# Other sizes for the seven pieces of a streaming kernel's last row

## Chip, cores and metric

The kernel runs on one core of a Trainium2 chip. The metric is the device time of one execution in microseconds (us).

## The reference

```python
log_input: float32 [1024, 4096]
target:    float32 [1024, 4096]

def reference(log_input, target):
    loss = np.exp(log_input) - target * log_input
    return np.mean(loss, axis=-1).astype(np.float32)
```

## The kernel before

Each of the 128 partitions holds eight rows of the batch. log_input (x) and target (t) stream in over one DMA queue. ScalarE takes exp(x) with its row sum, VectorE takes the product t*x with its row sum. The rows come in loads of four rows, two rows and one row; the last row comes in seven pieces, so that the arithmetic left after the last byte is small. A unit in this text is 32 columns, a 128th of a row, 16 KB over 128 partitions; "x98" is an x piece of 98 units.

```python
TAIL = [("x", 98), ("t", 50), ("t", 48), ("x", 24), ("t", 18), ("x", 6), ("t", 12)]
# ... cut: views, buffers, semaphores
for what, w in TAIL:
    loads.append((what, at[what], w * d // 128))
    at[what] += w * d // 128
# ... cut: all loads are issued in this order from SyncE, each with its own semaphore;
#     the last t load, the last exponential and the last but one product all count last_ready up
# VectorE, for each t piece (lo, w, i):
    x_load = next(ix for a, wx, ix in x_work if a + wx >= lo + w)   # the x piece that covers it
    if j == 0 or x_load > t_work[j - 1][2]:
        nc.vector.wait_ge(landed[x_load], 16)
    if j < n_t - 1:
        nc.vector.tensor_tensor_reduce(...).wait_op(landed[i], 16, "sem-ge")     # L175
    else:   # the last product also adds up the six partial sums of the row
        # ... cut: waits for the earlier partial sums
        nc.vector.tensor_tensor_reduce(...).wait_op(last_ready, 18, "sem-ge")    # L193
```

Of the kernel before, what the change touches and what calls it, by code (L numbers as in the profile page):

```python
# [7 lines left out]
F32 = mybir.dt.float32  # L8


TAIL = [("x", 98), ("t", 50), ("t", 48), ("x", 24), ("t", 18), ("x", 6), ("t", 12)]


def before_first_barrier(nc, instructions):
# [16 lines left out]
def kernel(tc, log_input, target, out):  # L31
# [33 lines left out]
    at = {"x": last_row * d, "t": last_row * d}  # L65
    for what, w in TAIL:
        loads.append((what, at[what], w * d // 128))
# [175 lines left out]
```

## Time and profile before

| | before |
|---|---|
| time, three runs | 84.07 us (84.00 to 84.13) |
| span of the profiled run | 82.5 us |
| VectorE, ScalarE busy | 43%, 40% |
| DMA queue busy | 95.8% |

How to read it: in the profile DVE is VectorE, ACT is ScalarE, SPq is SyncE's queue of DMA issues; a READ_ACCUMULATOR line, one column wide, follows each product (0.08 us) and each exponential (0.19 us), for which the kernel asks for a row sum. Both engines idle for more than half of the span, and the queue hardly at all, so shares say nothing about the tail; only start times do. In the timeline a line has the start, the duration, the engine and source line, the operation, and in brackets the idle time before it with what ended it. Three lines that the prediction does not show serve below as marks: the first product of the whole kernel, the product of the row before the last, and the exponential of the last row's large x piece.

```profile
41.12 4.43 DVE L175 CUSTOM_DVE_ANT_0 t_big<-t_big,x_big 128x4096 f32<-128x4096 f32 x1 [41.12 <-DMA t_big<-in_target_dram]
...
70.33 4.43 DVE L175 CUSTOM_DVE_ANT_0 t_big<-t_big,x_big 128x4096 f32<-128x4096 f32 x1 [1.00 <-DMA t_big<-in_target_dram]
...
74.10 2.79 ACT L155 ACTIVATE e_dump<-x_big 128x3136 f32<-128x3136 f32 x1 [4.44 <-DMA x_big<-in_log_input_dram]
```

All three start when their load lands. They tell when the stream reached a given byte in this run.

### The profile page before, as it was taken

How to read it: one execution, taken by the hardware profiler on the slowest of the kernel's cores; microseconds unless marked ns; L12 is line 12 of the kernel's file. 1: busy time of each engine (PE TensorE's matmuls, PEld its weight loads, DVE VectorE, ACT ScalarE, POOL GpSimd, SP SyncE). 2: the span in 40 equal slices, each digit the busy share in tenths (PEclk: the TensorE clock that was granted, in tenths of full speed). 3: DMA queues.
4: the chain of work that ended last, by engine and by line, in shares of the span. 5: the costliest groups of instructions: out<-in, count | busy, mean ns of one | idle time of the engine just before them, and what ended most of it. 6: DMA issues, size and time to landing. Idle time of an engine off the chain costs nothing.

```text
span 82.5 us, 131 instructions
## 1 busy us (share of the span) xinstructions
DVE 35.6 (43%) x22; ACT 33.2 (40%) x35; POOL 0.3 (0%) x5
## 2 busy tenths in 40 slices
DVE  0000000000000000000099999999369995993992
ACT  0500000000499920000000998979792496009460
POOL 0000000000000000000000000000000000000000
DMA  9289999929999992999599799799799999999960
GB/s 508 127 381 508 508 508 508 476 95 445 508 508 508 508 413 95 508 508 508 254 508 429 333 508 492 318 460 508 302 453 397 461 421 418 426 402 412 397 231 2
DMA packets 2016, 33.56 MB, mean 407 GB/s; under 512 B 352, under 2 KB 608, under 8 KB 1120
## 3 DMA queue, kind: packets, MB, share of 16 engines
q1 hardware_dynamic: 2016, 33.56, 95.8%
HBM read 33.55 MB, written 0.00 MB: 407 GB/s over the span
## 4 chain that ended last, share of the span: by engine, by line
DMA 72%; DVE 18%; issue 5%; SPq 3%; DVEq 0%
DMA t_big<-in_target_dram 49%; DMA x_big<-in_log_input_dram 23%; DVE t_big L175 17%; SPq L129 3%; DVE t_big L193 1%; DVE parts L175 0%; DVEq L192 0%; SPq L127 0%; DVE all_loss L193 0%
## 5 line engine op out<-in xcount | busy, mean ns | idle before, releaser
L175 DVE CUSTOM_DVE_ANT_0 t_big<-t_big,x_big 128x4096 f32<-128x4096 f32 (+3 forms) x8 | 26.2, 3308 | 43.5 <-DMA t_big<-in_target_dram 43.4
L155 ACT ACTIVATE e_dump<-x_big 128x4096 f32<-128x4096 f32 (+3 forms) x8 | 21.8, 2729 | 23.9 <-DMA x_big<-in_log_input_dram 23.6
L141 ACT ACTIVATE join_dump<-parts 128x2 f32<-128x2 f32 x7 | 1.4, 203 | 20.4 <-DVE parts L175 20.3
L175 DVE CUSTOM_DVE_ANT_0 t_mid<-t_mid,x_mid 128x4096 f32<-128x4096 f32 x2 | 8.8, 4424 | 2.0 <-DMA t_mid<-in_target_dram 2.0
L155 ACT ACTIVATE e_dump<-x_mid 128x4096 f32<-128x4096 f32 x2 | 7.1, 3568 | 0.0
L155 ACT ACT_TABLE_LOAD x1 | 1.3, 1283 | 2.9 <-PEq L48 2.9
L155 ACT ACTIVATION_READ_ACCUMULATOR e_dump<-x_big 128x1 f32 x8 | 1.5, 186 | 0.0
L141 ACT ACTIVATION_READ_ACCUMULATOR join_dump<-parts 128x1 f32 x7 | 1.3, 186 | 0.0
L175 DVE DVE_READ_ACCUMULATOR2_ANT parts<- 128x1 f32 x7 | 0.6, 84 | 0.0
L193 DVE CUSTOM_DVE_ANT_0 t_big<-t_big,x_big 128x390 f32<-128x390 f32 x1 | 0.6, 566 | 0.0
L155 ACT ACTIVATION_READ_ACCUMULATOR e_dump<-x_mid 128x1 f32 x2 | 0.4, 186 | 0.0
L175 DVE DVE_READ_ACCUMULATOR2_ANT t_big<- 128x1 f32 x3 | 0.2, 82 | 0.0
L136 POOL MEMSET x_big<- 128x6 f32 x1 | 0.1, 104 | 2.5 <-POOLq L48 2.5
L227 POOL MEMSET const-uint8-127<- 128x1 uint8 x1 | 0.1, 102 | 0.0
L227 POOL MEMSET const-bfloat16-1.0<- 128x1 bf16 x1 | 0.1, 101 | 0.0
L227 POOL MEMSET const-float32-0.0<- 128x1 f32 x1 | 0.1, 98 | 0.2 <-issue 0.2
L227 POOL MEMSET const-float32-1.0<- 128x1 f32 x1 | 0.1, 98 | 0.0
L193 DVE DVE_READ_ACCUMULATOR2_ANT all_loss<- 128x1 f32 x1 | 0.1, 82 | 0.0
## 6 DMA issues: line engine op xcount, KB each, us to landing
x_mid<-in_log_input_dram SPq DMA_DIRECT2D x1, 4096.0 KB, 49.9
t_mid<-in_target_dram SPq DMA_DIRECT2D x1, 4096.0 KB, 59.2
x_big<-in_log_input_dram SPq DMA_DIRECT2D x1, 2048.0 KB, 19.8
t_big<-in_target_dram SPq DMA_DIRECT2D x1, 2048.0 KB, 24.3
x_big<-in_log_input_dram SPq DMA_DIRECT2D x1, 1568.0 KB, 15.4
t_big<-in_target_dram SPq DMA_DIRECT2D x1, 800.0 KB, 17.0
t_big<-in_target_dram SPq DMA_DIRECT2D x1, 768.0 KB, 18.4
x_big<-in_log_input_dram SPq DMA_DIRECT2D x1, 384.0 KB, 18.9
```

Of the source, the lines that this page charges most:

```text
L129: dma = nc.sync.dma_start(out=place(what, lo, w), in_=src[:, lo : lo + w])
L136: nc.gpsimd.memset(big["x"][:, 4 * d : 4 * d + n_parts], -1.0).then_inc(ones_done, 1)
L141: nc.scalar.activation(out=join_dump[:, 2 * row : 2 * row + 2], in_=parts[:, 2 * row : 2 * row + 2], func=ACT_F.Copy, scale=inv_d, accum_o ...
L155: nc.scalar.activation(out=e_dump[:, col : col + w], in_=place("x", lo, w), func=ACT_F.Exp, bias=0.0, scale=1.0, accum_out=parts[:, 2 * ro ...
L175: nc.vector.tensor_tensor_reduce(out=place("t", lo, w), in0=place("t", lo, w), in1=place("x", lo, w), scale=-1.0, scalar=0.0, op0=ALU.mult ...
L193: nc.vector.tensor_tensor_reduce(out=place("t", lo, w + n_parts), in0=place("t", lo, w + n_parts), in1=place("x", lo, w + n_parts), scale= ...
L227: nc = _bacc.Bacc("TRN2", target_bir_lowering=False, num_devices=1)
```

## The change

Only the sizes of the last row's pieces change; their order, their number and their total stay. To judge by the sizes, the intent is rounder pieces: all x pieces (3200, 768 and 128 columns of 4 bytes) become whole multiples of 512 bytes a partition.

```diff
-TAIL = [("x", 98), ("t", 50), ("t", 48), ("x", 24), ("t", 18), ("x", 6), ("t", 12)]
+TAIL = [("x", 100), ("t", 50), ("t", 50), ("x", 24), ("t", 16), ("x", 4), ("t", 12)]
```

## The prediction

> **What bounds the kernel now.** I read the page first. ScalarE and VectorE are each busy for well under half of the span, and the DMA queue carries 33.56 MB at almost its full share, so the kernel is a stream of loads with the arithmetic beside it:
>
> ```profile
> span 82.5 us, 131 instructions
> DVE 35.6 (43%) x22; ACT 33.2 (40%) x35; POOL 0.3 (0%) x5
> q1 hardware_dynamic: 2016, 33.56, 95.8%
> ```
>
> The change alters neither the bytes nor the number of loads, so the body of the stream cannot gain. What can move is the short stretch at the end, in which the last row arrives in seven pieces. The page's list of issues gives the time from issue to landing, and the chain in order of time gives the issue times 59.06, 59.53, 60.02, 60.52 and 61.04; the timeline has the first issue (x of 98 units) at 58.69 and the last at 61.52. (A unit is 32 columns, one 128th of a row, so 16 KB over 128 partitions.)
>
> ```profile
> x_big<-in_log_input_dram SPq DMA_DIRECT2D x1, 1568.0 KB, 15.4
> t_big<-in_target_dram SPq DMA_DIRECT2D x1, 800.0 KB, 17.0
> t_big<-in_target_dram SPq DMA_DIRECT2D x1, 768.0 KB, 18.4
> x_big<-in_log_input_dram SPq DMA_DIRECT2D x1, 384.0 KB, 18.9
> t_big<-in_target_dram SPq DMA_DIRECT2D x1, 288.0 KB, 19.2
> t_big<-in_target_dram SPq DMA_DIRECT2D x1, 192.0 KB, 18.9
> x_big<-in_log_input_dram SPq DMA_DIRECT2D x1, 96.0 KB, 18.9
> ```
>
> Adding the two gives landings, each good to about 0.05 us: x98 74.09, t50 76.06, t48 77.93, x24 78.92, t18 79.72, x6 79.94, t12 80.42. Against these stands the timeline of the end (start, duration, instruction):
>
> ```profile
> 76.05 1.83 DVE L175 CUSTOM_DVE_ANT_0 t_big<-t_big,x_big 128x1600 f32<-128x1600 f32 x1 [1.28 <-DMA t_big<-in_target_dram]
> 77.80 0.08 DVE L175 DVE_READ_ACCUMULATOR2_ANT t_big<- 128x1 f32 x1
> 77.94 1.76 DVE L175 CUSTOM_DVE_ANT_0 t_big<-t_big,x_big 128x1536 f32<-128x1536 f32 x1
> 78.93 0.81 ACT L155 ACTIVATE e_dump<-x_big 128x768 f32<-128x768 f32 x1 [1.53 <-DMA x_big<-in_log_input_dram]
> 79.62 0.08 DVE L175 DVE_READ_ACCUMULATOR2_ANT t_big<- 128x1 f32 x1
> 79.68 0.19 ACT L155 ACTIVATION_READ_ACCUMULATOR e_dump<-x_big 128x1 f32 x1
> 79.70 0.76 DVE L175 CUSTOM_DVE_ANT_0 t_big<-t_big,x_big 128x576 f32<-128x576 f32 x1
> 79.97 0.33 ACT L155 ACTIVATE e_dump<-x_big 128x192 f32<-128x192 f32 x1
> 80.24 0.19 ACT L155 ACTIVATION_READ_ACCUMULATOR e_dump<-x_big 128x1 f32 x1
> 80.38 0.08 DVE L175 DVE_READ_ACCUMULATOR2_ANT t_big<- 128x1 f32 x1
> 80.50 0.57 DVE L193 CUSTOM_DVE_ANT_0 t_big<-t_big,x_big 128x390 f32<-128x390 f32 x1
> ```
>
> What to see: the product of t48 starts at 77.94, just as its data land, 0.06 us after the previous accumulator read ended (77.88). From there VectorE runs without a hole that matters: 77.94 to 79.70, 79.70 to 80.46, and the last instruction at 80.50. That last one waits for three things at once, and all three come within 0.04 us: ScalarE's last read (80.24 + 0.19 = 80.43), the landing of t12 (80.42) and VectorE's own previous piece (80.46). The old sizes balance the tail so finely that anything moved later on one of the three arms shows in full, while moving one of them earlier gains nothing.
>
> [...]
>
> **The change part by part.** It adds no instruction and removes none. Every piece still needs the same x loads, there are still six partial sums, and t12 with its 390-column last instruction is as before.
>
> *Landings.* From x98's landing (74.10, where its exponential starts) to t48's (77.94) 800 + 768 KB came in 3.84 us, which is 418 GB/s, or 0.039 us for a unit. All loads run through one queue in order of issue, so a landing moves by the change in the sum of units up to it. The sums were 98, 148, 196, 220, 238, 244, 256 and become 100, 150, 200, 224, 240, 244, 256. So x100 and the first t50 land 0.08 us later, the second t50 0.16 later, x24 0.16 later, t16 0.08 later, and x4 and t12 where x6 and t12 did.
>
> *VectorE.* The first t50 starts at 76.05 + 0.08 = 76.13 and is over, accumulator read and all, at 77.96 (1.83 later). The second t50 lands at 77.93 + 0.16 = 78.09, so VectorE now stands still for some 0.1 us and starts at 78.10. It has 1600 columns for 1536, 1.826 us for 1.759 (the two durations on the page), and ends at 79.93. t16 has landed at 79.80 and starts at once. [...] It ends at 80.62. The last instruction starts 0.04 us later, as before, at 80.66 for 80.50.
> The sum is simpler than the steps: from the second large t piece on VectorE works through 1536 + 576 = 2112 columns before and 1600 + 512 = 2112 after, in the same number of instructions. So the shift of the end is the shift of that piece's landing, 4 units x 0.039 = 0.16 us; the 64 columns that the piece gained are given back by t16.
>
> *ScalarE.* x24 starts at 78.93 + 0.16 = 79.09 and its read at 79.84. The next ACTIVATE can start 0.09 us after a read has started (45.70 and 45.79 in the timeline), at 79.93; x4 lands only at 79.94, so it starts at 79.97 as x6 did. [...] so its read ends at about 80.38 instead of 80.43. This arm gets 0.05 us shorter, which buys nothing.
>
> *Path that sets the end.* VectorE 80.62, t12 80.42, ScalarE 80.38. VectorE alone sets it, +0.16 us. The output store and the rest follow unchanged. 84.07 + 0.16 = 84.23 us, +0.19%.
>
> **Rivals.**
> 1. The stream sets the end, the time stays at 84.07. For it: the DMA queue is 95.8% busy, and t12 lands where it did. Against it: in the tail VectorE has no slack, its own piece ended 0.04 us after t12 landed already before. It would need the second t50 to start early, and it cannot, for it starts on landing.
> 2. ScalarE becomes the last arm: x24 is late, its read pushes x4. By the steps above there is 0.01 us between read and landing, so a small delay of x24 does pass on. But x4 would have to start 0.25 us late to pass VectorE (80.38 + 0.25 = 80.63). An extra delay of that size would bring some 84.3; I see nothing that causes it.
> 3. The transfers get faster or slower with the sizes. The two middle pieces now end at multiples of 512 B in the row (3200 columns are 12800 B, 3136 were 12544 B), and the small ones are 2048 and 512 B. The tail already runs below 418 GB/s in its small pieces (96 and 288 KB between 78.92 and 79.94, which is 386 GB/s), so size matters a little. If round sizes helped by a few per cent on the 200 units up to the second t50, which take 8 us, it would land 0.1 to 0.2 us earlier and the result would be 84.0 to 84.1[...]. Against it: the first t50 (6400 B, not a multiple of 512) and t48 (6144 B, one) came at the same rate, 800 KB in 1.95 us and 768 KB in 1.89, 420 and 416 GB/s.
>
> **Range and chances.** The three runs of before lie within 0.13 us, as large as the effect, and the landings are known to 0.05 us. With rivals 1 and 3 on the low side and 2 and 3 on the high side I take 84.03 to 84.42. Two per cent are 1.68 us, ten times the largest shift found in any arm, so within 2% has 0.98, and the rest is split evenly.
>
> **What would show it.** In the profile after: t products of 1600, 1600, 512 and 390 columns at some 1826, 1826, 692 and 566 ns; a wait of about 0.1 us on the target's load before the second 1600; no wait before the 512; the last instruction about 0.2 us after ScalarE's last read and after t12's landing, released by VectorE's own read. Wrong would be a last instruction that starts at 80.5 with the second 1600 no later than 77.96 (then the landings did not move by units), or one that waits for ScalarE or for t12's load.

The forecast's sum came to 84.07 + 0.16 = 84.23 us, with VectorE at 80.62 ahead of t12 (80.42) and ScalarE (80.38); two of its terms are 0.692 us for the product of 512 columns and 0.281 us for the exponential of 128. Both can be estimated from the profile of before alone (`--lines --by-form`). Products of 1600, 1536 and 576 columns took 1826, 1759 and 759 ns, so a column costs (1826 - 1759)/64 = 1.047 ns and 512 columns 759 - 64 x 1.047 = 692 ns. Exponentials of 768 and 192 columns took 815 and 334 ns, so a column costs 481/576 = 0.835 ns and 128 columns 334 - 64 x 0.835 = 281 ns.

## The result

| | before | after |
|---|---|---|
| median of six runs | 84.02 us (83.98 to 84.13) | 84.14 us (83.98 to 84.22) |
| ratio after/before | | 1.0011, 95% interval 0.9998 to 1.0024 |
| span of the profiled run | 82.5 us | 82.8 us |

A ratio is the mean time of one kernel's fast runs over that of the other's of the same rounds, so it is not quite the ratio of the medians quoted. The clock alone does not settle that anything changed: the interval reaches to 1. The profile does, if it is read with care. The same lines of the timeline of the changed kernel:

```profile
41.31 4.43 DVE L175 CUSTOM_DVE_ANT_0 t_big<-t_big,x_big 128x4096 f32<-128x4096 f32 x1 [41.31 <-DMA t_big<-in_target_dram]
...
70.53 4.43 DVE L175 CUSTOM_DVE_ANT_0 t_big<-t_big,x_big 128x4096 f32<-128x4096 f32 x1 [1.01 <-DMA t_big<-in_target_dram]
...
74.37 2.84 ACT L155 ACTIVATE e_dump<-x_big 128x3200 f32<-128x3200 f32 x1 [4.52 <-DMA x_big<-in_log_input_dram]
...
76.33 1.82 DVE L175 CUSTOM_DVE_ANT_0 t_big<-t_big,x_big 128x1600 f32<-128x1600 f32 x1 [1.37 <-DMA t_big<-in_target_dram]
...
78.08 0.08 DVE L175 DVE_READ_ACCUMULATOR2_ANT t_big<- 128x1 f32 x1
78.29 1.82 DVE L175 CUSTOM_DVE_ANT_0 t_big<-t_big,x_big 128x1600 f32<-128x1600 f32 x1
...
80.04 0.08 DVE L175 DVE_READ_ACCUMULATOR2_ANT t_big<- 128x1 f32 x1
80.04 0.69 DVE L175 CUSTOM_DVE_ANT_0 t_big<-t_big,x_big 128x512 f32<-128x512 f32 x1
80.18 0.28 ACT L155 ACTIVATE e_dump<-x_big 128x128 f32<-128x128 f32 x1
80.40 0.19 ACT L155 ACTIVATION_READ_ACCUMULATOR e_dump<-x_big 128x1 f32 x1
80.65 0.08 DVE L175 DVE_READ_ACCUMULATOR2_ANT t_big<- 128x1 f32 x1
80.77 0.57 DVE L193 CUSTOM_DVE_ANT_0 t_big<-t_big,x_big 128x390 f32<-128x390 f32 x1
```

The last product starts at 80.77 for 80.50, 0.27 us later. But the first product of the kernel, far ahead of anything that changed, already starts 0.19 us later (41.31 for 41.12). That part is the stream of this one run. What is left for the change is 0.27 - 0.19 = 0.08 us.

A better mark lies closer: the start of the large exponential, at which x98 or x100 has landed. The time from there to the last product is 80.50 - 74.10 = 6.40 us before and 80.77 - 74.37 = 6.40 after; x100 is two units larger and so should itself land 2 x 0.039 = 0.08 us later (0.039 us a unit is 3.84 us for 98 units, from 74.10 to 77.94 before), which puts it at 6.48 on the scale of before. Again +0.08 us, but all of it is this correction, so it has to be checked: from the product of the row before to the large exponential it is 74.10 - 70.33 = 3.77 us before and 74.37 - 70.53 = 3.84 after, 0.07 more.

The landings moved as the prediction said. In the list of issues (us from issue to landing) the two t50 pieces now share one line with their median, and t12 has the other:

```profile
t_big<-in_target_dram SPq DMA_DIRECT2D x2, 800.0 KB, 17.8
...
t_big<-in_target_dram SPq DMA_DIRECT2D x1, 192.0 KB, 19.0
```

t12, issued at 61.68, landed at 80.68, which is 10.15 us after the product of the row before it started (70.53); before it was 80.42 - 70.33 = 10.09. The list gives these times to 0.1 us, so each landing is good to 0.05 us. The packed trace keeps the landings themselves to the nanosecond: 10.11 us in both kernels. It did not move. The second t50 started at 78.29, 0.13 us after the previous accumulator read had ended (78.08 + 0.08), so it did wait for its load.

What the prediction did not see is the pair of lines at 80.04: the 512-column product starts together with the accumulator read before it. In the kernel before the same pair stands at 79.62 and 79.70. There t18 waited for its load and started 0.08 us after VectorE could have taken it. The landing records of the trace agree: t18 landed 0.05 us after that read had started, and its product started 0.02 us after the landing. In the changed kernel t16 landed 0.06 us before the read started, so its product had nothing to wait for.

### The profile page after: what moved, and what is told of

Its sections match the earlier page's. It is cut to its first block, busy times and chain, and to the rows that moved or that the text cites. A ratio compares the mean times of both kernels' runs of the same rounds, so it can differ in the third digit from the quotient of the medians.

```text
span 82.8 us, 131 instructions
## 1 busy us (share of the span) xinstructions
DVE 35.5 (43%) x22; ACT 33.1 (40%) x35; POOL 0.3 (0%) x5
## 4 chain that ended last, share of the span: by engine, by line
DMA 72%; DVE 19%; issue 6%; SPq 1%; DVEq 0%
DMA t_big<-in_target_dram 72%; DVE t_big L175 19%; SPq L129 1%; DVE t_big L193 1%; DVE parts L175 0%; DVEq L192 0%; SPq L127 0%; DVE all_loss L193 0%
## 5 line engine op out<-in xcount | busy, mean ns | idle before, releaser
L175 DVE CUSTOM_DVE_ANT_0 t_big<-t_big,x_big 128x4096 f32<-128x4096 f32 (+2 forms) x8 | 26.2, 3306 | 43.8 <-DMA t_big<-in_target_dram 43.7
## 6 DMA issues: line engine op xcount, KB each, us to landing
x_big<-in_log_input_dram SPq DMA_DIRECT2D x1, 1600.0 KB, 15.5
```

The source lines that it names most:

```text
L175: nc.vector.tensor_tensor_reduce(out=place("t", lo, w), in0=place("t", lo, w), in1=place("x", lo, w), scale=-1.0, scalar=0.0, op0=ALU.mult ...
```

## The experiments

**Two theories.** P is the prediction: the end moves by the whole shift of the second large t piece's landing, 0.039 us a unit. H (the hole), formed from the two profiles before the first experiment: a product that waits for nothing starts with the accumulator read ahead of it, so before t18 there was a hole of 0.08 us, and the first 0.08 us of any delay ahead of it disappears in it. Rivals are R (the round sizes alter the rate of the transfers) and plain noise. Every experiment changes the one line TAIL of the kernel before, and every one gave a correct result.

How the shift of the end is measured here: from the start of the large exponential to the start of the last product, plus 0.039 us for each unit of the first x piece over 98 (minus for units under), less 6.415, the mean of the two profiles of the kernel before (6.40 and 6.43). The correction is the same for P and H, so it does not decide between them: without it, P asks for 0.08, 0.16 and 0.23 us more in the single, double and triple change, H for 0.00, 0.08 and 0.16. The expectations count from the issue of the first x piece instead. I changed that mark after seeing the first run, for a reason shown there; the table at the end gives both, and a third that needs no correction: the time from t12's landing, as the trace records it, to the last product. The units up to t12 are the same in every version with seven pieces.

### e1, the changed kernel again

```diff
+TAIL = [("x", 100), ("t", 50), ("t", 50), ("x", 24), ("t", 16), ("x", 4), ("t", 12)]
```

> The changed kernel once more. Theory P (the prediction): the end moves by the whole shift of the second large t piece's landing, 4 units x 0.039 = +0.16 us. Theory H (the hole): in the kernel before, VectorE stood idle for 0.08 us between the start of the accumulator read of t48 (79.62) and the start of t18 (79.70), because t18 had only just landed; in the changed kernel the 512-column piece starts together with that read (80.04 and 80.04), so 0.08 of the 0.16 is absorbed and the end moves by +0.08 us. Measured from the issue of the row's first x piece to the last instruction: 21.81 before, P 21.97, H 21.89. Ratio: P 1.0019, H 1.0009.

By the clock 84.08 us, ratio 1.0007 (0.9983 to 1.0030). From the first x issue (58.63) to the last product (81.06) it is 22.43 us, which fits neither theory. The cause lies ahead of the tail: the product of the row before started 12.02 us after that issue (70.65), where the first profile had 11.65, and x100 took 16.0 us from issue to landing for 15.5. The first profile of this kernel had 80.77 - 58.88 = 21.89 by the same mark, just what H said; the same program's stream differed by half a microsecond between two profiled runs. From the exponential at 74.64 it is 6.42, with the correction 6.50, a shift of +0.09 us (the first profile of this kernel: 6.48, +0.07). The 512-column product again starts with the read before it (80.32 and 80.32). H, not P.

### e2, the x sizes alone

```diff
+TAIL = [("x", 100), ("t", 50), ("t", 48), ("x", 24), ("t", 18), ("x", 4), ("t", 12)]
```

> Only the x sizes of the change (100, 24, 4), the t sizes of before (50, 48, 18, 12). The sums of units up to the second large t piece and up to t18 both grow by 2, so t48 and t18 both land 0.08 us later; t18 still waits for its landing, nothing is absorbed. P and H both: +0.08 us, last instruction 21.89 after the issue of the first x piece, ratio 1.0009. H adds that this is the same time as the whole change, so that the t part costs nothing on top; P says the whole change is 0.08 slower than this run.

By the clock 84.00 us, ratio 0.9990 (0.9971 to 1.0009), which sees nothing. In the profile the last product starts 21.91 us after the first x issue, and 80.71 - 74.29 = 6.42 after the exponential, corrected 6.50: +0.09 us, as much as the whole change. t18 waits for its load (its start 79.91, the read before it 79.83): the hole is still there, for everything moved together. Three profiles have x100 and need no correction against each other: 6.42 here, 6.40 and 6.42 with the t part on top, where P asked for 0.08 more. So the x part alone gives the shift, and the t part costs nothing: the 0.08 us that the second t50 lands later goes into the hole.

### e3, the t sizes alone

```diff
+TAIL = [("x", 98), ("t", 50), ("t", 50), ("x", 24), ("t", 16), ("x", 6), ("t", 12)]
```

> Only the t sizes of the change (50, 50, 16, 12), the x sizes of before (98, 24, 6). The second t piece now needs columns 3136 to 3200, which come with x24, so VectorE waits for x24 (about 79.0) in place of its own load (78.0). From there 1600, 512 and 390 columns follow without a gap. P and H both: first start of the second piece 78.99, end +1.0 us, ratio 1.012. If the x piece did not matter (the target's load alone released it), +0.05 us or less.

By the clock 85.02 us, ratio 1.0115 (1.0093 to 1.0137). The timeline:

```profile
79.06 0.81 ACT L155 ACTIVATE e_dump<-x_big 128x768 f32<-128x768 f32 x1 [1.62 <-DMA x_big<-in_log_input_dram]
79.17 1.83 DVE L175 CUSTOM_DVE_ANT_0 t_big<-t_big,x_big 128x1600 f32<-128x1600 f32 x1 [1.24 <-DMA x_big<-in_log_input_dram]
...
81.65 0.57 DVE L193 CUSTOM_DVE_ANT_0 t_big<-t_big,x_big 128x390 f32<-128x390 f32 x1
```

The second t piece stands still for 1.24 us and is released by an x load, not by its own: its last 64 columns come with x24. The shift is 81.65 - 74.14 - 6.415 = +1.10 us, 0.1 more than expected; ScalarE starts on the same landing at 79.06 and VectorE only at 79.17; why it starts 0.11 us later was not tested. So t48 cannot grow to t50 alone: the first x piece must cover the pair of large t pieces.

### e4, the change doubled

```diff
+TAIL = [("x", 102), ("t", 50), ("t", 52), ("x", 24), ("t", 14), ("x", 2), ("t", 12)]
```

> The change doubled: x 102, t 50, t 52, x 24, t 14, x 2, t 12. The second large t lands 8 units later, 0.31 us; columns on VectorE from there on are the same 2112. P: +0.31 us, ratio 1.0037, last instruction 22.12 after the first x issue. H: 0.31 - 0.08 = +0.23 us, ratio 1.0027, 22.04. ScalarE's x2 is at the limit, its last read ends at about the same time as VectorE's less 0.2. Rival R (round sizes alter the rate of the transfers): x2 is 256 B a partition; [...] t12 lands later than 21.73 after the first x issue, by 0.1 or more.

By the clock 84.16 us, ratio 1.0028 (0.9996 to 1.0061). The timeline:

```profile
80.14 0.08 DVE L175 DVE_READ_ACCUMULATOR2_ANT t_big<- 128x1 f32 x1
80.14 0.62 DVE L175 CUSTOM_DVE_ANT_0 t_big<-t_big,x_big 128x448 f32<-128x448 f32 x1
...
80.81 0.57 DVE L193 CUSTOM_DVE_ANT_0 t_big<-t_big,x_big 128x390 f32<-128x390 f32 x1
```

The third piece starts with the read. The last product starts 22.07 us after the first x issue (80.81 - 58.74; H said 22.04, P 22.12, which does not decide), and (80.81 - 74.32) + 0.16 = 6.65 after the exponential: +0.23 us. H said 0.23, P 0.31. Against R: x2 is a piece of 256 bytes a partition, and t12 behind it landed at 61.53 + 19.0 = 80.53, 10.14 us after the product of the row before (70.39), against 10.09 before. By the landings kept in the trace it is 10.13, and 10.10 in e6, which has an x2 too, against 10.11 before and 10.09 in e5. The 0.1 us in t12 that the expectation set for R, a guess of mine and from no run, is not there. Only x2 itself is late: by the trace it landed at 9.71 us in e4 and 9.70 in e6, where x6, with the same sum of units, had landed at 9.62 and 9.63 in the two profiles of before. ScalarE has time to spare there (its last read ends 0.32 us before the last product starts in e4, 0.44 in e6), so this does not reach the end.

### e5, the kernel before again

No edit; the kernel before under a new name.

> The kernel before, once more, for what a profile and five rounds of the same program differ by. Ratio 1.000 within 0.001. In the profile: the stream's first products may start anywhere within some 0.2 us (41.12 and 41.31 in the two profiles so far); but from the first x issue of the last row to the last instruction it should be 21.81 within 0.04 us, and t18 should again start 0.08 after the accumulator read before it has started (H needs this hole to be there each time).

By the clock 83.95 us, ratio 0.9986 (0.9969 to 1.0004) against itself. So in this setting 0.1% by the clock is within what the same program shows, and the single change (0.08 of 84 us) is below what five rounds can resolve. The profile repeats to 0.05 us: first x issue to last product 21.86 us (0.05 above the first profile, where 0.04 was expected), exponential to last product 6.43. The hole is there again: the read at 79.64, t18 at 79.74, 0.10 us.

### e6, the change three times as large

```diff
+TAIL = [("x", 104), ("t", 50), ("t", 54), ("x", 22), ("t", 12), ("x", 2), ("t", 12)]
```

> The change three times as large: x 104, t 50, t 54, x 22, t 12, x 2, t 12. The second large t lands 12 units later, 0.47 us; again the same columns after it. P: +0.47 us, ratio 1.0056. H: 0.47 - 0.08 = +0.39 us, ratio 1.0046; last instruction 22.20 after the first x issue (P 22.28). Noise alone as the cause: no growth from the single change to this one.

By the clock 84.34 us, ratio 1.0030 (1.0012 to 1.0049). This time the interval leaves out 1, so the growth with the shift shows by the clock too. It also leaves out 1.0056 (P) and holds 1.0046 (H), but that does not decide between them: e5 was at 0.9986 with no edit at all, which is more than the 0.0010 that separates the two. The profile separates them. The timeline:

```profile
78.49 1.96 DVE L175 CUSTOM_DVE_ANT_0 t_big<-t_big,x_big 128x1728 f32<-128x1728 f32 x1 [0.30 <-DMA t_big<-in_target_dram]
...
80.38 0.08 DVE L175 DVE_READ_ACCUMULATOR2_ANT t_big<- 128x1 f32 x1
80.38 0.55 DVE L175 CUSTOM_DVE_ANT_0 t_big<-t_big,x_big 128x384 f32<-128x384 f32 x1
...
80.97 0.57 DVE L193 CUSTOM_DVE_ANT_0 t_big<-t_big,x_big 128x390 f32<-128x390 f32 x1
```

The wait for the second t load has grown to 0.30 us, and the third piece again starts with the read. From the first x issue 22.21 us; from the exponential (74.40) 6.57 + 0.23 = 6.80, a shift of +0.39 us. H said 0.39, P 0.47.

### e7, the change turned round

```diff
+TAIL = [("x", 96), ("t", 50), ("t", 46), ("x", 24), ("t", 20), ("x", 8), ("t", 12)]
```

> The change turned round: x 96, t 50, t 46, x 24, t 20, x 8, t 12. The second large t lands 0.16 us earlier, t20 0.08 earlier, t12 as before. Taken by the landing alone (P without its other arms): -0.16 us. By the balance of three arms: t20 starts on landing at about 79.58, its 640 columns end 80.41, t12 lands at 80.42, ScalarE's x8 takes 0.39 from 79.95 and its last read ends at 80.47, so the last instruction starts at 80.50 to 80.52, +0.00 to +0.03 us, ratio 1.000, and it is ScalarE that holds it.

By the clock 83.99 us, ratio 0.9998 (0.9975 to 1.0021). The shift is 80.58 - 74.07 - 0.08 - 6.415 = +0.02 us. The timeline:

```profile
80.36 0.19 ACT L155 ACTIVATION_READ_ACCUMULATOR e_dump<-x_big 128x1 f32 x1
80.42 0.08 DVE L175 DVE_READ_ACCUMULATOR2_ANT t_big<- 128x1 f32 x1
80.58 0.57 DVE L193 CUSTOM_DVE_ANT_0 t_big<-t_big,x_big 128x390 f32<-128x390 f32 x1
```

ScalarE's read ends at 80.55, VectorE's at 80.50, the last product starts 0.03 us after ScalarE. The chain of the profile (`--critical`) ends in x8's landing, ScalarE and the last product. So the arm changed and, by this mark, the end did not: the large pieces' earlier landings buy nothing, because x8 takes ScalarE 0.06 us longer than x6 (0.39 us for 0.33). By the mark on record it is 21.96 us, 0.10 to 0.15 more than before. The landings in the trace show why the two marks differ: from x96 on, every load landed some 0.1 us later after the product of the row before than the sums of units say, so, as in e1, the stream lost time ahead of the tail. This is one profile; the shift rests on taking that loss out.

### e9, a wider hole

```diff
+TAIL = [("x", 98), ("t", 52), ("t", 46), ("x", 24), ("t", 18), ("x", 6), ("t", 12)]
```

> The kernel before with two units moved from the second t piece to the first: x 98, t 52, t 46, x 24, t 18, x 6, t 12. The second piece starts where t48 did (77.94 to 77.96), now when VectorE comes free and its load lands together, and has 1472 columns in place of 1536, so its accumulator read starts 0.07 us earlier than t48's. t18 lands when it did. P (from the second large piece on only VectorE's columns count): the last instruction 0.07 us earlier. H (t18 starts on landing): the gap between the start of that read and the start of t18 grows from 0.08 to about 0.14 us and the end stays, 0.00 us; from the start of the 3136-column exponential to the last instruction 6.40 to 6.43 as before (P 6.35). The wall time cannot tell the two apart, the profile can.

By the clock 84.05 us, ratio 1.0006 (0.9986 to 1.0027). The timeline:

```profile
74.17 2.79 ACT L155 ACTIVATE e_dump<-x_big 128x3136 f32<-128x3136 f32 x1 [4.44 <-DMA x_big<-in_log_input_dram]
...
79.64 0.08 DVE L175 DVE_READ_ACCUMULATOR2_ANT t_big<- 128x1 f32 x1
...
79.80 0.76 DVE L175 CUSTOM_DVE_ANT_0 t_big<-t_big,x_big 128x576 f32<-128x576 f32 x1
...
80.60 0.57 DVE L193 CUSTOM_DVE_ANT_0 t_big<-t_big,x_big 128x390 f32<-128x390 f32 x1
```

VectorE has 64 columns less to do from the second large piece on (that piece takes 1.69 us for 1.76), the gap between the read and t18 grows to 0.16 us, and the time from the exponential to the last product is 6.43, as in e5. P's rule of counting columns would give 6.35. The hole is real, and it is the landing of t18 that ends it (issued at 60.58, 19.2 us to landing: 79.78).

### e8 and e10, a tail of eight pieces

```diff
+TAIL = [("x", 95), ("t", 53), ("t", 42), ("x", 22), ("t", 19), ("x", 11), ("t", 6), ("t", 8)]
```

> A try at a faster tail with one more piece: x 95, t 53, t 42, x 22, t 19, x 11, t 6, t 8. The last product has 256 + 7 columns in place of 384 + 6, 0.13 us shorter, for one more load [...] . Worked out with the landings and durations of before: -0.07 us, ratio 0.9991. If the extra load or the extra product costs more than 0.13 us, it is slower than before.

> The tail of eight pieces a second time, for whether its gain repeats: x 95, t 53, t 42, x 22, t 19, x 11, t 6, t 8. In the first run ratio 0.9967 by the clock, while the kernel before, resubmitted in the same call, came out at 0.9986 against itself. Expected 0.998, -0.12 to -0.2 us, from the last product's 263 columns for 390 (0.13 us) and a VectorE chain without holes. If the first result was chance, 1.000.

By the clock 83.79 us, ratio 0.9967 (0.9948 to 0.9986), and the second time 83.90 us, ratio 0.9980 (0.9967 to 0.9993). The second timeline:

```profile
79.58 0.08 DVE L175 DVE_READ_ACCUMULATOR2_ANT t_big<- 128x1 f32 x1
79.58 0.79 DVE L175 CUSTOM_DVE_ANT_0 t_big<-t_big,x_big 128x608 f32<-128x608 f32 x1
...
80.69 0.43 DVE L193 CUSTOM_DVE_ANT_0 t_big<-t_big,x_big 128x263 f32<-128x263 f32 x1
```

There is no hole ahead of the third t piece, the last product starts 80.69 - 74.14 - 0.12 = 6.43 us after the exponential (on the scale of before, 6.42 in e8), no later than before, and takes 0.43 us in place of 0.57. That is -0.14 us, about 0.0017 of 84 us. It lies within both intervals, and both lie below 1. The first run gained more than the 0.9991 that it was expected to: the sum of that expectation, -0.07 us, held beside the shorter last product (-0.13 us) a small delay for the additional load, which was my guess. By the trace the last load landed at 10.04 us after the product of the row before in both runs, where t12 had landed at 10.11 and 10.09. It was run twice because e5 had come out at 0.9986 with no edit. This version is the fastest, and by a margin that no one would notice.

### The shifts in one table

| | units that the second t piece lands later | P | H | from the large exponential, corrected | from t12's landing | mark on record, us | ratio by the clock |
|---|---|---|---|---|---|---|---|
| before; e5 | 0 | | | -0.01; +0.01 | -0.03; +0.03 | 21.81; 21.86 | 0.9986 (e5) |
| after; e1 | 4 | +0.16 | +0.08 | +0.07; +0.09 | +0.05; +0.05 | 21.89; 22.43 | 1.0011; 1.0007 |
| e2, x alone | 2 | +0.08 | +0.08 | +0.09 | +0.09 | 21.91 | 0.9990 |
| e4, double | 8 | +0.31 | +0.23 | +0.23 | +0.21 | 22.07 | 1.0028 |
| e6, triple | 12 | +0.47 | +0.39 | +0.39 | +0.37 | 22.21 | 1.0030 |
| e9, wider hole | 0 | -0.07 | 0.00 | +0.02 | +0.02 | 21.85 | 1.0006 |
| e7, turned round | -4 | -0.16 | 0.00 to +0.03 (three arms) | +0.02 | +0.02 | 21.96 | 0.9998 |

The column from t12's landing is the shift against the mean of before (0.06 us) and e5 (0.11 us). It is good to about the 0.05 us between these two, and it agrees with H in every row and with P in none but e2, where the two say the same.

## Why the prediction was right, and where it was not

**The bound and the direction** were right. The kernel is a stream, no instruction came or went, and the end moved by a tenth of a per cent: 84.14 us against 84.23 predicted, inside 84.03 to 84.42. That range also holds 84.07, no change at all, so the hit says little about the mechanism; of the forecast shift of 0.16 us the profiles show half.

**Landings by sums of units** were right. The second t50 landed late enough to make VectorE wait (0.13 us, predicted about 0.1), t12 did not move, and doubling and tripling the shift gave waits (0.21 and 0.30 us) and ends on the line.

**Durations** were right: 1824 ns for the two products of 1600 columns (predicted 1826), 686 for 512 (692, the estimate beside the prediction), 567 for the last (566); ScalarE's 128 columns took 282 ns (281, likewise).

**The step that failed** is "from there VectorE runs without a hole that matters", and with it "the shift of the end is the shift of that piece's landing". The term was 0.16 us and measured 0.07 and 0.09. The missing half is the 0.08 us between the read at 79.62 and t18 at 79.70. I had both lines in the prediction, and took the end of the accumulator read, 79.70, as the moment at which VectorE comes free. In these traces it is free for the next product when the read starts (80.04 and 80.04, 80.32 and 80.32); only the last product, which waits for the product before it by the code, starts 0.12 us after that read has started (80.65 to 80.77; 80.38 to 80.50 before). And t18's own landing, worked out as 79.72 to 0.05 us, had been the cause of the wait. In the sum, 1.826 us from the start of the second t50 to that of the 512-column product was too long: it is 1.75 (78.29 to 80.04; 78.57 to 80.32 in e1). e4, e6 and e9 separate the two readings; e2 shows that the t part of the change was free.

**ScalarE** stayed off the end, as predicted (its last read ended 0.18 us ahead of the last product; predicted 0.28), and so did t12's load (landed 0.14 us ahead; predicted 0.24). In e7, the reverse, it did become the last arm.

**Rivals.** The stream alone (no change) is excluded by the series up to e6. Sizes that alter the rate did not show in the change: by the trace all seven landings of the changed kernel lie within 0.03 us of what the sums of units say. Only the piece of 256 bytes a partition, in e4 and e6, was itself 0.08 us late, and even there t12 landed where it did, within 0.03 us. That the single change itself costs time is read from its two profiles and from the series; its own timing does not show it, for the intervals hold 1.

## What to carry to other kernels

When a chain of instructions on one engine looks unbroken, compare each start with the earliest start that the engine allows. For these products that was the start, not the end, of the accumulator read before (80.04 and 80.04 in the changed kernel). The hole of 0.08 us here absorbed the first part of a delay (in e6 0.39 us of 0.47, by sums of units, reached the end), and earlier work went into idle time (in e9 the hole grew to 0.16 us and the end stayed). Before comparing the ends of two profiles, subtract what already differs at a mark ahead of the change: here 0.19 of 0.27 us was the run's own. To see an effect below the noise of the clock, scale it up two and three times and look whether it grows on the line.
